# First norm of a hybrid decoder trunk: column sums and the modulation's shift with the data as the stationary operand, and eight load buffers of their own

## The chip, the cores and the metric

The kernel runs on one core of one Trainium2 chip. The metric is the device time of one execution in microseconds; the time before is the median of three runs. The core has five engines: TensorE (PE; PEld is its weight load), VectorE (DVE), ScalarE (ACT), GpSimd (POOL) and SyncE (SP), which issues most of the DMAs. Each works through its own instructions in a fixed order and waits on semaphores for the others.

## The reference, cut to what matters

A decoder trunk of two layers over a sequence of 1024 tokens with 1024 features. Layer 0 mixes with an S5 state space, layer 1 with Mamba-2; a squared-ReLU MLP follows each. Every sublayer starts with a norm and a modulation by a conditioning vector c:

```
def _rmsnorm(x, g):
    y = xf * lax.rsqrt(jnp.mean(xf * xf, axis=-1, keepdims=True) + NORM_EPS)
    return y * g
def _modulate(h, shift, scale):
    return h * (1 + scale) + shift
...
cond = jax.nn.silu(c)
mod = cond @ ada_w[i] + ada_b[i]
sh1, sc1, g1, sh2, sc2, g2 = jnp.split(mod[:, None, :], N_MOD, axis=-1)
h = _modulate(_rmsnorm(x, norm_mix_g[i]), sh1, sc1)
y = _s5_mixer(h, ...)
```

The change concerns the first `_rmsnorm` of layer 0, and `sh1` and `sc1` of its first `_modulate`.

## The kernel before, in words

Activations lie transposed: features on the 128 partitions, tokens along the free axis. x is eight tiles `x0[k]` of 128 features by 1024 tokens, each seen as two halves `x[k][f]` of 512 tokens.

The head of the program, up to the first projection, does this:

- `mod_rows` loads c on all partitions and makes `cond`; `mod_setup` makes `condc`, the same values with feature k*128+p in column k.
- `rstd_first` (L182) loads the eight x tiles, squares each half on ScalarE (L190) and sums over the partitions on TensorE (L191): the weight is `ones` (128x1), the 512 squares stream, and the result is one row per half, accumulated over k. `columns` (L337) then copies the two rows to SBUF (L341) and turns them into eight columns `pn` by eight products with one column (L344). VectorE makes `rfv` from them (L194), then the inverse root in some dozen small operations (`rsqrt`, L137 to L143, tiles `rsi`, `rst`, `rfy`), and `spread` (L156) broadcasts the result over the partitions.
- `mod_block` (L306) makes the scale: eight rows `ada` of 512 KB are loaded (L332), each multiplied with `cond` and summed by one VectorE operation (L333, the dot). At its end stand `mod` (L316) and `G` (L322), the factor of the norm.
- `mod_shift` (L347) makes the shift: eight tiles `ada` from `in_ada0` (L354) stream through TensorE against a column of `condc` (L356) into two rows, and `columns` turns these into eight columns; L361 writes them to `K.mod`.
- Both load into the pool `raw` with four buffers, which c (`craw`), the first weights and other tiles use as well. The scale's loop runs ahead, and from its fifth step one step of the shift is taken for each step of the scale.
- Then x is scaled with G (L1516, 16 operations), and `shift_split` writes each of the 16 tiles h as a high part on ScalarE (L237) and the rest on VectorE (L238). x holds both halves until then.
- `s5_uproj` projects h with `s5_w_in`: each unit of weights is loaded (L95) and split into `whi` (ScalarE, L84) and `wlo` (VectorE, L85), and three products per block (L117 whi by h high, L118 whi by h low, L119 wlo by h high) go to TensorE. `s5_tables`, `s5_front` (L896 on VectorE; `dI` and `bb` are its first results; L945 and L946 on TensorE) and `s5_back` prepare the state space beside it.

The order of instructions on each engine isn't written by hand: a scheduler fixes it when the kernel is built, by its own model of the times, so that work from further down (the tables of the state space, such as `mag`, `q`, `R`) stands between the operations above. Once built, it doesn't change. Tiles take their buffers from pools, and a buffer that is still in use makes the next load wait.

Of the kernel before, what the change touches and what calls it, by code (L numbers as in the profile page):

```python
# [11 lines left out]
F32 = mybir.dt.float32  # L12
# [7 lines left out]
P = 128  # L20
# [3 lines left out]
KT = D // P  # L24
# [28 lines left out]
def half_of(half):  # L53
    return slice(half * HT, half * HT + HT)


def blk(i, n=P):
    return slice(i * n, i * n + n)
# [4 lines left out]

def psum(K):

    K.turn += 1
    i = K.turn % (6 if K.wide else 4)
    if i >= 4:
        return K.pw.tile([P, 512], F32, tag="pw", name="pd")
    return (K.ps if i < 2 or not K.psb else K.psb).tile([P, 512], F32, tag="ps", name="pd")  # L70


def psw(K):

    return K.pw.tile([P, 512], F32, tag="pw", name="pm")


def tmp(K, name):
    return K.tmp.tile([P, 512], F32, tag="t", bufs=6, name=name)
# [51 lines left out]
def rsqrt(K, y, v):  # L131

    V = K.nc.vector
    n = v.shape[1]
    i = K.tmp.tile([P, n], I32, tag="rsi", name="rsi")
    t = K.tmp.tile([P, n], F32, tag="rst", name="rst")
    V.tensor_scalar(i, v.bitcast(I32), 1, None, op0=ALU.logical_shift_right)  # L137
    V.tensor_scalar(i, i, -1, 0x5F3759DF, op0=ALU.mult, op1=ALU.add)
    yy = i.bitcast(F32)
    for _ in range(3):  # L140
        V.scalar_tensor_tensor(t, yy, -0.5, yy, op0=ALU.mult, op1=ALU.mult)
        V.tensor_tensor(t, t, v, op=ALU.mult)
        V.scalar_tensor_tensor(y, t, 1.5, yy, op0=ALU.add, op1=ALU.mult)  # L143
        yy = y


def pss(K):

    return K.pss.tile([P, 512], F32, tag="pss", name="pn")


def spread(K, y, bank=pss):

    pb = bank(K)
    for j in range(4):
        K.nc.tensor.matmul(pb[:, blk(j)], y[:, j:j + 1].to_broadcast([P, P]), K.ident, start=True, stop=True)  # L156
    return pb
# [23 lines left out]

def rstd_first(K, x, load):  # L182

    nc = K.nc
    pr = [psw(K), psw(K)]
    for k in range(KT):
        load(k)
        for f in range(2):
            sq = tmp(K, "sq")
            nc.scalar.activation(sq, x[k][f], AF.Square)  # L190
            nc.tensor.matmul(pr[f][0:1], K.ones, sq, start=k == 0, stop=k == KT - 1)  # L191
    pt = columns(K, pr, 8)
    v = K.tmp.tile([P, 8], F32, tag="rfv", name="rfv")
    nc.vector.tensor_scalar(v, pt[:, 0:8], 1.0 / D, EPS, op0=ALU.mult, op1=ALU.add)  # L194
    y = K.tmp.tile([P, 8], F32, tag="rfy", name="rfy")
    rsqrt(K, y, v)
    return [spread(K, y[:, f * 4:f * 4 + 4], psw) for f in range(2)]
# [36 lines left out]
def shift_split(K, t, h, sh):  # L234

    hi, lo = h
    K.nc.scalar.activation(hi, t, AF.Identity, bias=sh)  # L237
    K.nc.vector.scalar_tensor_tensor(lo, t, sh, hi.bitcast(F32), op0=ALU.add, op1=ALU.subtract)  # L238
# [8 lines left out]
def h_half(K, h, half):  # L247
    for k in range(KT):
        h[k][half] = (h_tile(K, k, half, 0), h_tile(K, k, half, 1))


def h_new():
    return [[None, None] for _ in range(KT)]
# [23 lines left out]
def drain(gen):  # L277
    for _ in gen:
        pass
# [26 lines left out]
def mod_block(K, ada, i, j):  # L306

    nc = K.nc
    o = i * 48 + j * 8
    acc = K.tmp.tile([P, 8], F32, tag="macc", name="macc")  # L310
    for k in range(8):
        mod_dot(K, ada[i, j * 8 + k], acc[:, k:k + 1])
        if k < 7:
            yield
    m = K.mod[:, o:o + 8]
    nc.vector.scalar_tensor_tensor(  # L316
        m, acc, 0.5, K.cst[:, C_ADAB + o:C_ADAB + o + 8], op0=ALU.mult, op1=ALU.add
    )
    if j in (1, 4):
        s = i * 2 + (j == 4)  # L320
        g0 = (C_GMLP if j == 4 else C_GMIX) + i * 8
        nc.vector.scalar_tensor_tensor(  # L322
            K.G[:, s * 8:s * 8 + 8], m, 1.0, K.cst[:, g0:g0 + 8], op0=ALU.add, op1=ALU.mult
        )
    yield


def mod_dot(K, w, acc):

    pool, bufs = (K.adap, 2) if K.adap else (K.raw, 4)  # L330
    r = pool.tile([P, 1024], F32, tag="ada" if K.adap else "raw", name="ada", bufs=bufs)
    K.nc.sync.dma_start(r, w)  # L332
    K.nc.vector.scalar_tensor_tensor(r, r, 1.0, K.cond, op0=ALU.mult, op1=ALU.mult, accum_out=acc)  # L333


def columns(K, rows, n):

    nc = K.nc
    row = K.wt.tile([P, 1024], F32, tag="whi", name="row")
    for f, r in enumerate(rows):  # L340
        nc.scalar.copy(row[0:1, half_of(f)], r[0:1])  # L341
    pt = pss(K)
    for j in range(n):
        nc.tensor.matmul(pt[:, j:j + 1], row[0:1, blk(j)], K.ones[0:1], start=True, stop=True)  # L344
    return pt


def mod_shift(K, w):

    nc = K.nc  # L350
    rows = [psum(K), psum(K)]
    for k in range(KT):
        r = K.raw.tile([P, 1024], F32, tag="raw", name="ada")
        nc.sync.dma_start(r, w[k])  # L354
        for f in range(2):
            nc.tensor.matmul(  # L356
                rows[f][0:1], K.condc[:, k:k + 1], r[:, half_of(f)], start=k == 0, stop=k == KT - 1
            )
        yield
    pt = columns(K, rows, 8)  # L360
    nc.vector.scalar_tensor_tensor(  # L361
        K.mod[:, 0:8], pt[:, 0:8], 0.5, K.cst[:, C_ADAB:C_ADAB + 8], op0=ALU.mult, op1=ALU.add
    )


def mod_gate(K, ada, k):

    V = K.nc.vector
    acc = K.tmp.tile([P, 1], F32, tag="mac1", name="mac1")
    mod_dot(K, ada[0, 16 + k], acc)  # L370
    m = K.mod[:, 16 + k:17 + k]
    V.scalar_tensor_tensor(m, acc, 0.5, K.cst[:, C_ADAB + 16 + k:C_ADAB + 17 + k], op0=ALU.mult, op1=ALU.add)
    V.tensor_scalar(K.g1h[:, k:k + 1], m, 0.5, None, op0=ALU.mult)
# [409 lines left out]
def s5_tables(K, keep, pool, Lm):  # L783
# [4 lines left out]

    nc, V, S = K.nc, K.nc.vector, SimpleNamespace()

# [3 lines left out]
    def KT_(nm, n=64):  # L794
        return keep.tile([P, n], F32, name=nm, tag=nm, bufs=1)
# [3 lines left out]
    for nm, top, bot in (("1", 0.25, 0.0), ("2", 0.5, 0.25)):  # L799
# [4 lines left out]
        o[nm] = (t, b)  # L804
    S.sgn, S.nsgn, S.quarter = KT_("sgn", 1), KT_("nsgn", 1), KT_("quarter", 1)
    V.memset(S.sgn[0:64], 1.0)
    V.memset(S.sgn[64:128], -1.0)
    V.tensor_scalar(S.nsgn, S.sgn, -TWO_PI, None, op0=ALU.mult)
    V.memset(S.quarter, TWO_PI / 4)

# [594 lines left out]
@with_exitstack  # L1405
def trunk(ctx: ExitStack, tc: tile.TileContext, io, out):
    nc = tc.nc
    K = SimpleNamespace(nc=nc, tc=tc, io=io, turn=-1, psb=None, wide=False, adap=None, nact=7)

    def perm(name, **kw):  # L1410
        return ctx.enter_context(tc.tile_pool(name=name, **kw))
# [26 lines left out]
    def right(name, n=1):  # L1438
        return tc.alloc_tile_pool(name=name, bufs=n, side="right", reuse_waits="tile")
# [62 lines left out]
    t5 = right("tab5")  # L1502
    Lm = t5.tile([P, 3, 64], F32, name="lam", tag="lam", bufs=1)
    nc.sync.dma_start(Lm, io.lam.rearrange("a p g -> p a g"))
    pb = rstd_first(K, x, lambda k: nc.sync.dma_start(x0[k], io.x[k]))
    shift, scale = mod_shift(K, io.ada0), mod_block(K, io.ada, 0, 1)
    for k in range(KT):
        next(scale)
        if k >= 4:
            next(shift)  # L1510
    drain(shift)
    h = h_new()
    for f in range(2):
        h_half(K, h, f)
        for k in range(KT):
            nc.vector.scalar_tensor_tensor(x[k][f], x[k][f], K.G[:, k:k + 1], pb[f], op0=ALU.mult, op1=ALU.mult)  # L1516
        for k in range(KT):
            shift_split(K, x[k][f], h[k][f], K.mod[:, k:k + 1])
    S = s5_tables(K, keep5, t5, Lm)
    t5.release()  # L1520
    xp.release()
# [107 lines left out]
    pr = ssd_proj(K, cp, h, 0)  # L1629
# [27 lines left out]
    for gr in range(1, 4):  # L1657
        pr = ssd_proj(K, cp, h_mix, gr)
# [123 lines left out]
```

## Time and profile before

| | |
|---|---|
| median of three runs | 2531.93 us (2530.64 to 2536.54) |
| profiled execution, its own time | 2533.94 us |
| span of its profile | 2532.2 us |
| mean granted TensorE clock | 0.986 |
| PE busy | 2451.7 us (97%) |
| DVE busy | 1914.6 us (76%) |
| ACT busy | 1167.9 us (46%) |
| DMA | 503.80 MB, mean 199 GB/s |

Times in the profile's rows are microseconds from the start of the span. A row of the timeline has start, duration, engine, line, operation, what it writes and reads, shapes and count, and in brackets the idle time of the engine before it and what ended it. In the chain of work that ended last each row has start, duration and what the chain went through. Matmuls are pipelined and their ends are modelled, so the distance between starts tells more of the pace than a duration does. An f32 product appears as two passes. The granted clock (PEclk) is 1.00 at full speed and 0.50 at half.

### The profile page before, as it was taken

To read this page: it belongs to the slowest core of one execution; us is meant where nothing else is said; L and a number is where in the kernel's file an instruction comes from. 1 tells how busy PE (TensorE), PEld (TensorE's weight loads), DVE (VectorE), ACT (ScalarE), POOL (GpSimd) and SP (SyncE) were. 2 spreads that over 40 slices of the span, in tenths; PEclk is the share of its full clock that TensorE was granted. 3 is DMA by queue.
4 is the path that set the end of the run, shared out by engine and by line. 5 is a ranking of instruction groups with operands and counts; after the bars stand their busy time and mean duration, and the time that the engine had idled before them with its cause. 6 is when DMAs were issued, how large, how long until landed. Compare 5 with 4: busy or idle time off the path is not lost.

```text
span 2532.2 us, 32780 instructions
## 1 busy us (share of the span) xinstructions
PE 2451.7 (97%) x11624; PEld 1965.7 (78%) x11624; DVE 1914.6 (76%) x3265; ACT 1167.9 (46%) x1955; POOL 213.7 (8%) x400
## 2 busy tenths in 40 slices
PE   7999999999998999999999999999999999899997
PEld 2788788877776888777888878778888777688886
DVE  8798754967887997958596868789687777776664
ACT  4587412744444433534564655544255444444342
POOL 0010000112221000100000000000011222200000
PEclk9999999999999999999999999999999999999998
DMA  6576772467769979723455554584245666874752
GB/s 243 155 169 169 242 242 96 153 204 250 258 227 343 342 260 308 272 85 115 154 160 160 161 173 139 169 259 136 88 141 192 225 231 232 294 250 136 254 194 77
DMA packets 284645, 503.80 MB, mean 199 GB/s; under 512 B 22081, under 2 KB 162369, under 8 KB 284481
## 3 DMA queue, kind: packets, MB, share of 16 engines
q1 hardware_dynamic: 242496, 386.34, 47.3%
q0 software_dynamic: 32384, 106.98, 12.4%
q10 hardware_dynamic: 9600, 8.39, 1.0%
q8 instruction: 91, 1.49, 0.2%
q14 instruction: 74, 0.60, 0.1%
HBM read 364.27 MB, written 133.17 MB: 196 GB/s over the span
## 4 chain that ended last, share of the span: by engine, by line
PE 74%; issue 8%; DVE 6%; DMA 6%; ACT 4%; POOL 2%; SPq 0%; DVEq 0%; POOLq 0%; ACTq 0%
PE pd L118 10%; PE pd L117 10%; PE pd L119 10%; PE py L117 4%; PE py L118 4%; PE py L119 4%; PE px L117 3%; PE pm L117 2%; PE pm L118 2%; PE pm L119 2%; PE px L119 2%; PE px L118 2%; PE pv L117 2%; PE pv L118 2%; PE pv L119 2%
## 5 line engine op out<-in xcount | busy, mean ns | idle before, releaser
L84 ACT CAST whi<-raw 128x1024 fp32r<-128x1024 f32 x241 | 251.0, 1048 | 365.5 <-PE pd L118 146.3
L85 DVE TENSOR_TENSOR wlo<-raw,whi 128x1024 fp32r<-128x1024 f32 x241 | 293.2, 1218 | 113.6 <-ACT whi L84 110.2
L333 DVE SCALAR_TENSOR_TENSOR ada<-ada,cond 128x1024 f32<-128x1024 f32 x88 | 107.3, 1222 | 57.8 <-DMA ada<-in_ada 57.7
L498 ACT ACTIVATE s<-s 128x512 f32<-128x512 f32 x84 | 53.0, 631 | 158.5 <-DVE s L496 155.9
L390 POOL DMA_DIRECT2D hscr<-x x32 | 17.3, 541 | 953.6 <-DVE x L736 751.1
L1235 DVE SCALAR_TENSOR_TENSOR cacc<-cr,conv,cacc 128x1024 f32<-128x1024 f32 x72 | 91.7, 1279 | 0.9 <-ACT cacc L1216 0.8
L1288 ACT ACTIVATE L<-csb,cs 128x128 f32<-128x128 f32 x224 | 69.9, 391 | 38.4 <-DMA csb<-csr 33.7
L505 POOL DMA_DIRECT2D b<-s x96 | 51.8, 540 | 330.9 <-ACT s L499 281.7
L496 DVE TENSOR_TENSOR s<-s,px 128x512 f32<-128x512 f32 x60 | 41.0, 684 | 34.9 <-PE px L119 34.9
L496 DVE TENSOR_TENSOR s<-s,pv 128x512 f32<-128x512 f32 x36 | 24.7, 686 | 55.5 <-PE pv L119 55.5
L505 POOL DMA_DIRECT2D b<-tt x96 | 51.8, 540 | 43.0 <-DVE tt L510 25.8
L499 ACT ACTIVATE s<-s 128x512 f32<-128x512 f32 x84 | 53.2, 633 | 2.7
L1239 ACT ACTIVATE cth<-cacc 128x512 f32<-128x512 f32 x48 | 27.7, 625 | 41.4 <-DVE cacc L1235 41.3
L667 DVE SCALAR_TENSOR_TENSOR x<-py,mod,x 128x512 f32<-128x512 f32 x40 | 27.3, 744 | 25.6 <-PE py L119 25.6
L1215 ACT COPY cr<-pd 128x512 f32<-128x512 f32 x48 | 27.8, 579 | 35.0 <-PE pd L119 35.0
L1308 DVE SCALAR_TENSOR_TENSOR y<-xs,cst,pm 128x128 f32<-128x128 f32 x128 | 38.3, 342 | 4.8 <-PE pm L1305 4.8
L117 PE MATMUL pd<-h00h,whi 128*128 128x512 f32 (+1 forms) x97 | 39.7, 411 | 2.0 <-ACT h00h L237 1.8
L1106 ACT ACTIVATE gt<-pd,bgh 128x512 f32<-128x512 f32 x16 | 11.0, 685 | 65.5 <-PE pd L119 65.5
L117 PE MATMUL pd<-h01h,whi 128*128 128x512 f32 x97 | 39.4, 407 | 0.5 <-DVE h61h L736 0.5
L119 PE MATMUL pd<-h10h,wlo 128*128 128x512 f32 (+1 forms) x97 | 39.3, 405 | 0.0
L622 DVE TENSOR_TENSOR raw<-raw 128x1024 f32<-128x1024 f32 x16 | 19.6, 1225 | 26.0 <-DMA raw<-in_w 26.0
L118 PE MATMUL pd<-h00l,whi 128*128 128x512 f32 (+1 forms) x97 | 38.8, 400 | 0.4 <-DVE h00l L238 0.4
(996 smaller groups left out, 8173.0 us busy)
## 6 DMA issues: line engine op xcount, KB each, us to landing
raw<-in_w SPq DMA_DIRECT2D x204, 512.0 KB, 4.6
br<-b SPq DMA_DIRECT2D x112, 512.0 KB, 4.7
ada<-in_ada SPq DMA_DIRECT2D x96, 512.0 KB, 5.0
b<-s POOLq DMA_DIRECT2D x96, 256.0 KB, 2.9
b<-tt POOLq DMA_DIRECT2D x96, 256.0 KB, 3.8
csb<-csr SPq DMA_DIRECT2D x32, 512.0 KB, 4.5
raw<-in_w_xbc SPq DMA_DIRECT2D x24, 512.0 KB, 4.5
xscr<-cacc SPq DMA_DIRECT2D x24, 512.0 KB, 2.7
```

The source lines that it names most:

```text
L84: K.nc.scalar.copy(hi, src)
L85: K.nc.vector.tensor_tensor(lo, src, hi.bitcast(F32), op=ALU.subtract)
L117: K.nc.tensor.matmul(ps, wh, xh, start=start and i == 0, stop=False, skip_group_check=more)
L118: K.nc.tensor.matmul(ps, wh, xl, start=False, stop=False, skip_group_check=more)
L119: K.nc.tensor.matmul(ps, wl, xh, start=False, stop=stop and i == n - 1, skip_group_check=more)
L333: K.nc.vector.scalar_tensor_tensor(r, r, 1.0, K.cond, op0=ALU.mult, op1=ALU.mult, accum_out=acc)
L496: nc.vector.tensor_tensor(t, t, p, op=ALU.add)
L498: nc.scalar.activation(t, t, AF.Relu)
L499: nc.scalar.activation(t, t, AF.Square)
L505: self.K.nc.gpsimd.dma_start(self.bscr[DOWN.index(nm)][m // 2][m % 2], t)
L1235: V.scalar_tensor_tensor(acc, cr[:, t:t + L], K.cw[:, i, t:t + 1], acc, op0=ALU.mult, op1=ALU.add)
L1288: nc.scalar.activation(Lm[:, r, :], cb[:, r, :], AF.Relu, bias=S.cs[:, c0 + r:c0 + r + 1], scale=-1.0)
```

## The change

Three things change.

- `rstd_first` and `mod_shift` use the data as the stationary operand. `column` multiplies a 128x128 block of the squares (or of `ada`) as the weight with one moving column (`ones`, or a column of `condc`), and accumulates directly into a column of one PSUM tile `pn`. There are 64 such products in each place where there were 16. The rows, their copies and the function `columns` go.
- A pool `md` with eight buffers takes the loads of the scale and of the shift, in place of the four of `raw`. It stands on the right-hand stack above `tab5` and is released when h is made.
- The scale is now made whole, and then the shift, in place of the mixed loop.

```diff
-    pr = [psw(K), psw(K)]
+    pt = pss(K)
     for k in range(KT):
         load(k)
         for f in range(2):
             sq = tmp(K, "sq")
             nc.scalar.activation(sq, x[k][f], AF.Square)
-            nc.tensor.matmul(pr[f][0:1], K.ones, sq, start=k == 0, stop=k == KT - 1)
-    pt = columns(K, pr, 8)
+            for j in range(4):
+                column(K, pt, f * 4 + j, sq[:, blk(j)], K.ones, k == 0 and f == 0 and j == 0, k == KT - 1)
...
-    pool, bufs = (K.adap, 2) if K.adap else (K.raw, 4)
+    pool, bufs = (K.adap, K.nada) if K.adap else (K.raw, 4)
...
-def columns(K, rows, n):
+def column(K, pt, j, w, v, first, last):
+
+    K.nc.tensor.matmul(pt[:, j:j + 1], w, v, start=first, stop=last, skip_group_check=True)
...
-    rows = [psum(K), psum(K)]
+    pt = pss(K)
     for k in range(KT):
-        r = K.raw.tile([P, 1024], F32, tag="raw", name="ada")
+        r = K.adap.tile([P, 1024], F32, tag="ada", name="ada", bufs=K.nada)
         nc.sync.dma_start(r, w[k])
-        for f in range(2):
-            nc.tensor.matmul(
-                rows[f][0:1], K.condc[:, k:k + 1], r[:, half_of(f)], start=k == 0, stop=k == KT - 1
-            )
+        for j in range(KT):
+            column(K, pt, j, r[:, blk(j)], K.condc[:, k:k + 1], k == 0 and j == 0, k == KT - 1)
         yield
-    pt = columns(K, rows, 8)
...
+    K.adap, K.nada = right("md"), 8
     pb = rstd_first(K, x, lambda k: nc.sync.dma_start(x0[k], io.x[k]))
-    shift, scale = mod_shift(K, io.ada0), mod_block(K, io.ada, 0, 1)
-    for k in range(KT):
-        next(scale)
-        if k >= 4:
-            next(shift)
-    drain(shift)
+    drain(mod_block(K, io.ada, 0, 1))
+    drain(mod_shift(K, io.ada0))
...
+    K.adap.release()
+    K.adap, K.nada = None, 2
```

The scheduler lays the instructions anew. On TensorE, at the start of the program (`pm`, `pn`, `pd` are PSUM tiles; each row is one product or a run of them):

```order
L191 MATMUL pm<-sq,ones 1x512 x16
L344 MATMUL pn<-ones,row 128x1 x8
L356 MATMUL pd<-ada,condc 1x512 x3
L156 MATMUL pm<-ident,rfy 128x128 x8
L356 MATMUL pd<-ada,condc 1x512 x13
L344 MATMUL pn<-ones,row 128x1 x8
L117 MATMUL pd<-h00h,whi 128x512
L118 MATMUL pd<-h00l,whi 128x512
```

and in the changed kernel:

```order
L339 MATMUL pn<-ones,sq 128x1 x64
L156 MATMUL pm<-ident,rfy 128x128 x8
L339 MATMUL pn<-condc,ada 128x1 x64
L117 MATMUL pd<-h00h,whi 128x512
L118 MATMUL pd<-h00l,whi 128x512
L117 MATMUL pd<-h01h,whi 128x512
L118 MATMUL pd<-h01l,whi 128x512
L119 MATMUL pd<-h00h,wlo 128x512
```

The sums and the shift are 64 products with one column each (L339, one line for both), all of the shift stands behind the spread (L156), and the first projection takes the two halves' whi products ahead of the first product with wlo.

On VectorE, where the first dot stands (L333, L334 in the changed kernel), before:

```order
L333 SCALAR_TENSOR_TENSOR ada,macc<-ada,cond 128x1024
L833 TENSOR_TENSOR mag<-mag,ea_e_559 128x64
L880 TENSOR_TENSOR q_644<-nr,lam 128x64
L833 TENSOR_TENSOR mag<-mag,ea_e_559 128x64
L333 SCALAR_TENSOR_TENSOR ada,macc<-ada,cond 128x1024
L833 TENSOR_TENSOR mag<-mag,ea_e_559 128x64
L881 TENSOR_TENSOR qt_645<-ni,lam 128x64
L833 TENSOR_TENSOR mag<-mag,ea_e_559 128x64
L882 TENSOR_TENSOR q_644<-q_644,qt_645 128x64
L333 SCALAR_TENSOR_TENSOR ada,macc<-ada,cond 128x1024
L833 TENSOR_TENSOR mag<-mag,ea_e_559 128x64
```

and in the changed kernel:

```order
L334 SCALAR_TENSOR_TENSOR ada,macc<-ada,cond 128x1024
L195 TENSOR_SCALAR rfv<-pn 128x8
L824 TENSOR_TENSOR mag<-mag,ea_e_633 128x64
L137 TENSOR_SCALAR rsi<-rfv 128x8
L871 TENSOR_TENSOR q_718<-nr,lam 128x64
L138 TENSOR_SCALAR rsi<-rsi 128x8
L334 SCALAR_TENSOR_TENSOR ada,macc<-ada,cond 128x1024
L141 SCALAR_TENSOR_TENSOR rst<-rsi 128x8
L824 TENSOR_TENSOR mag<-mag,ea_e_633 128x64
L142 TENSOR_TENSOR rst<-rst,rfv 128x8
L872 TENSOR_TENSOR qt_719<-ni,lam 128x64
L143 SCALAR_TENSOR_TENSOR rfy<-rst,rsi 128x8
```

`rfv`, which reads the sums, moved from behind the third dot to right behind the first; the other seven dots stand behind it, and the operations of the inverse root between them.

On ScalarE, from the last squares on, before:

```order
L190 ACTIVATE sq<-x_247 128x512 x2
L341 COPY row<-pm 1x512 x2
L341 COPY row<-pd 1x512
L84 CAST whi<-raw 128x1024
L341 COPY row<-pd 1x512
L84 CAST whi<-raw 128x1024
L237 ACTIVATE h00h<-x_240,mod 128x512
L237 ACTIVATE h10h<-x_241,mod 128x512
```

and in the changed kernel, from the last high parts of h on:

```order
L238 ACTIVATE h51h<-x_245,mod 128x512
L238 ACTIVATE h61h<-x_246,mod 128x512
L238 ACTIVATE h71h<-x_247,mod 128x512
L84 CAST whi<-raw 128x1024 x2
L982 ACTIVATE tph<-iota,phi 128x128 x8
L918 COPY F_824<-BC 64x128
```

The two casts `whi` of the projection's first weights moved from ahead of the 16 high parts of h to behind them; the four row copies are gone. The first two `wlo` on VectorE stand behind the last low part of h as well, where one of them stood ahead of the first.

SyncE issues the eight loads of the scale and then the eight of the shift; before, it issued five of the scale, then shift and scale in turn, and five of the shift at the end. What it issues next (`s5d`, two `raw`, two `kscr`) stands as before.

More of the change, by code (lines that the diff above doesn't have):

```diff
@@ L333, in mod_dot @@
     K.nc.vector.scalar_tensor_tensor(r, r, 1.0, K.cond, op0=ALU.mult, op1=ALU.mult, accum_out=acc)
-def columns(K, rows, n):
[L338 to L345, printed above, removed]
+def column(K, pt, j, w, v, first, last):
+    K.nc.tensor.matmul(pt[:, j:j + 1], w, v, start=first, stop=last, skip_group_check=True)
 def mod_shift(K, w):
     nc = K.nc
-    rows = [psum(K), psum(K)]
+    pt = pss(K)
     for k in range(KT):
-        r = K.raw.tile([P, 1024], F32, tag="raw", name="ada")
+        r = K.adap.tile([P, 1024], F32, tag="ada", name="ada", bufs=K.nada)
         nc.sync.dma_start(r, w[k])
-        for f in range(2):
-            nc.tensor.matmul(
-                rows[f][0:1], K.condc[:, k:k + 1], r[:, half_of(f)], start=k == 0, stop=k == KT - 1
-            )
+        for j in range(KT):
+            column(K, pt, j, r[:, blk(j)], K.condc[:, k:k + 1], k == 0 and j == 0, k == KT - 1)
         yield
-    pt = columns(K, rows, 8)
     nc.vector.scalar_tensor_tensor(
@@ L1407, in trunk @@
     nc = tc.nc
-    K = SimpleNamespace(nc=nc, tc=tc, io=io, turn=-1, psb=None, wide=False, adap=None, nact=7)
+    K = SimpleNamespace(nc=nc, tc=tc, io=io, turn=-1, psb=None, wide=False, adap=None, nada=2, nact=7)
     def perm(name, **kw):
```

## The prediction

> **What bounds the kernel now.** I read the chain of work that ended last first, because only what stands on it costs time, and only its first 60 us, because the change touches nothing later by its own lines. Columns: start us, us, what.
>
> ```profile
> 24.76 4.63 DMA ada<-in_ada
> 29.52 3.59 PE pd L356 x4
> 33.13 6.03 DMA ada<-in_ada
> 39.20 1.89 PE pd L356 x4
> 41.10 4.72 DMA ada<-in_ada
> 45.87 4.47 PE pd L356 x10
> 51.88 0.48 ACT row L341
> 52.41 1.06 PE pn L344 x8
> 55.45 0.68 DVE h00l L238
> 56.17 0.79 PE pd L118
> ```
>
> From 24.76 to 53.5 the chain belongs to the shift: its loads, which come one by one because their buffers come free late, and its products (L356), then the row copies and columns (L341, L344). Then h is made and TensorE starts the input projection, in earnest at 56.17. Behind that, windows of 10 us (engine busy time and count for PE, PEld, DVE, ACT, POOL; granted clock; DMA share; GB/s):
>
> ```profile
> 100.00:110.00 10.00, 7.70 (x35) 6.02 (x34) 10.00 (x23) 6.82 (x15) 0.51 (x1) 0.84 0.98 246
> 110.00:120.00 10.00, 10.00 (x60) 7.57 (x59) 8.02 (x18) 5.53 (x9) 0.00 (x0) 0.99 0.28 95
> 190.00:200.00 10.00, 10.00 (x67) 8.90 (x66) 10.00 (x25) 7.84 (x13) 1.60 (x3) 1.00 0.96 209
> ```
>
> Apart from 2.3 us of idleness around 105, TensorE is full. So the head is worth what it moves the start of the projection on TensorE, less what a later start can fill up again.
>
> **What the products cost.** Old and new products move the same data through TensorE in opposite roles. The old ones stream 512 columns against a one-column weight:
>
> ```profile
> 8.27 15.38 PE L191 MATMUL pm<-sq,ones 128*1 128x512 f32 x32 [8.27 <-ACT sq L190]
> 9.93 0.13 PEld L191 LDWEIGHTS pm<-sq,ones 128*1 128x1 f32 x1 [0.72 <-issue]
> 10.78 0.13 PEld L191 LDWEIGHTS pm<-sq,ones 128*1 128x1 f32 x1 [0.72 <-ACT sq L190]
> 11.90 0.08 PEld L191 LDWEIGHTS pm<-sq,ones 128*1 128x1 f32 x1 [0.34 <-issue]
> 12.33 0.08 PEld L191 LDWEIGHTS pm<-sq,ones 128*1 128x1 f32 x1 [0.34 <-issue]
> ```
>
> Each f32 product is two passes (32 for 16). A pass starts 0.85 us after the last at first (9.93 to 10.78) and 0.43 us after it once the clock is up (11.90 to 12.33). The new form, a 128x128 weight and one column moving, is already in the later norms:
>
> ```profile
> 434.70 1.05 PE L173 MATMUL pn<-ones,ss 128*128 128x1 f32 x8 [0.37 <-DVE ss L170]
> 2516.85 1.87 PE L215 MATMUL pn<-ones,ss 128*128 128x1 f32 x8 [3.83 <-DVE ss L210]
> 2516.66:2520.07 3.41, 1.87 (x8) 1.78 (x8) 1.25 (x8) 0.00 (x0) 0.00 (x0) 0.50 0.00 0
> ```
>
> Eight passes end after 1.05 us at full clock and 1.87 us where the window shows a clock of 0.50. Less the tail of the last pass (about 0.19 and 0.16), that is 0.107 and 0.214 us a pass. The change puts four times as many passes (128 for 32, twice), each a quarter as long: **at equal clock the work is equal**, 13.7 us each time at full clock and 27.4 us at half. So the clock decides. These are windows of 3.41 us, laid where the clock changes:
>
> ```profile
> 24.95:28.36 3.41, 0.57 (x6) 0.48 (x5) 3.41 (x11) 0.00 (x0) 0.00 (x0) 1.00 0.77 238
> 28.36:31.77 3.41, 2.25 (x3) 0.37 (x4) 3.37 (x15) 0.00 (x0) 0.00 (x0) 0.50 0.92 296
> 31.77:35.19 3.42, 3.23 (x5) 0.19 (x3) 2.16 (x10) 0.00 (x0) 0.00 (x0) 0.50 0.70 235
> 38.60:42.01 3.41, 2.14 (x5) 0.34 (x6) 1.50 (x4) 0.00 (x0) 0.00 (x0) 1.00 0.77 255
> 55.67:59.08 3.41, 3.00 (x8) 2.33 (x8) 3.41 (x6) 3.41 (x7) 0.00 (x0) 0.50 0.00 0
> ```
>
> A window with PE busy 0.57 is followed by half clock; 2.25 leaves it there; 3.23 and 3.00 lift it. In these windows it is passes of 512 columns that lift it. No row shows whether a long run of one-column passes does: with 128x128 weights, eight is the longest run. That is the unknown, with both ends measured per pass. I take **half clock**. In a one-column pass hardly anything streams; the time goes into the weight load. And the nearest row is the one at 2516.85: it starts after idleness, with no streaming beside it, as here, and ran at half clock (though its 1.87 us in the window would not have been enough by the rows above either way).
>
> [...]
>
> **The sum at half clock.** Rows of VectorE and ScalarE:
>
> ```profile
> 21.88 1.22 DVE L333 SCALAR_TENSOR_TENSOR ada<-ada,cond 128x1024 f32<-128x1024 f32 x1
> 23.02 0.27 DVE L833 TENSOR_TENSOR mag<-mag,ea_e 128x64 f32<-128x64 f32 x1
> 23.51 1.21 DVE L333 SCALAR_TENSOR_TENSOR ada<-ada,cond 128x1024 f32<-128x1024 f32 x1
> 33.69 0.17 DVE L143 SCALAR_TENSOR_TENSOR rfy<-rst,rfy 128x8 f32<-128x8 f32 x1
> 42.19 9.97 DVE L1516 SCALAR_TENSOR_TENSOR x<-x,G,pm 128x512 f32<-128x512 f32 x15
> 53.49 0.17 DVE L361 SCALAR_TENSOR_TENSOR mod<-pn,cst 128x8 f32<-128x8 f32 x1 [1.33 <-PE pn L344]
> 54.23 1.22 DVE L85 TENSOR_TENSOR wlo<-raw,whi 128x1024 fp32r<-128x1024 f32 x1
> 55.37 0.75 DVE L238 SCALAR_TENSOR_TENSOR h00l<-x,mod,h00h 128x512 fp32r<-128x512 f32 x1
> 65.31 0.75 DVE L238 SCALAR_TENSOR_TENSOR h71l<-x,mod,h71h 128x512 fp32r<-128x512 f32 x1
> 67.10 0.27 DVE L896 TENSOR_TENSOR dI<-ident,s5d 16x128 f32<-16x128 f32 x1
> 50.84 1.04 ACT L84 CAST whi<-raw 128x1024 fp32r<-128x1024 f32 x1
> 54.49 0.72 ACT L237 ACTIVATE h00h<-x,mod 128x512 fp32r<-128x512 f32 x1
> 63.70 0.71 ACT L237 ACTIVATE h71h<-x,mod 128x512 fp32r<-128x512 f32 x1
> ```
>
> 1. Sums: 8.27 + 128 x 0.214 = 35.7, against 23.65 (8.27 + 15.38) before. The row copies and columns behind them (L341, L344) go. ScalarE's squares now wait for TensorE (six buffers), and so does the first dot behind them, by some 2 us; the wait in step 2 hides both.
> 2. VectorE's rfv now stands right behind the first product with the condition (the dot), and is a wait: the seven other dots queue behind it from about 25 to 35.8. Until rfy follow 4 dots of 1.14 us (21.88 to 23.02) and 19 small ones of 0.16 (three from 23.02 to 23.51): 7.6 us, 43.4. Up to G it is the old stretch 21.88 to 33.86 (12.0 us, six dots), one dot longer, with 0.5 us (an estimate, four small operations) for mod and G: 13.6 us, 49.4.
> 3. Spread (L156), 16 passes of 128 columns at half clock, priced as the one-column pass: 3.4 us, 46.8.
> 4. Shift: 128 x 0.214 = 27.4, ending at 74.2. The scaling of x (15 in 9.97 us) ends at 59 and hides. The last dot ends by 48 and frees the last buffer; its load lands by 53 (4.63 us as in the chain), well before its passes at 71. So the eight buffers hide, and gain nothing here. mod at 74.3.
> 5. ScalarE makes all 16 h tiles, now ahead of both weight casts: 15 x 0.614 (54.49 to 63.70) + 0.6 + 1.0 = 10.8, first projection pass at 85.1. VectorE's 16 (0.663 each, 55.37 to 65.31) and the first wlo (1.22) end at 87. Four passes fit ahead of that wait where one did, worth 1.3 us. So TensorE's real start goes from 56.17 to about 85.7: **+29.5**. VectorE's next stage (dI) goes from 67.10 to 88: +21.
> 6. Given back: 2.3 us of idleness near 105 and, in the same row, 16% of lost clock over 10 us, 1.6 us: -4.
>
> Together +25.5 on the profiled 2533.94 us: 2559.4. The median of the three runs stands 2.0 lower, so **2557**. Ends: if VectorE's delay alone counted and 4 us more were filled up, +17 (2549); with nothing given back, +29.5 (2561). Behind 110 the schedule is also shuffled; with a full TensorE I cost that at nothing, 1 us either way.
>
> **Rivals.**
> *Full clock (W).* If one-column passes count as work, sums end at 23.7 as before, rfv follows at 23.8, rfy at 31.4, G at 37.4. TensorE has been idle since 23.7, so spread runs at half clock to 34.8. The shift is bound by its passes: 4 at half clock, then 0.107 each, 49.0. Loads keep up:
>
> ```profile
> 18.00:20.00 2.00, 2.00 (x6) 0.34 (x4) 1.90 (x8) 1.16 (x3) 0.00 (x0) 1.00 1.01 404
> ```
>
> At 404 GB/s a row of 0.52 MB takes 1.3 us; the first is there for the dot at 21.88, so seven more are by 31, and the last dot (36.9) plus 4.63 is 41.5. mod at 49.1 is 4.4 us earlier than 53.49, but the late casts and the wlo eat it: wlo at 61.9, less 1.3, is +4.4 on TensorE, less the 4 given back: about 0, **2532** (2528 to 2538). For it: TensorE's rows are unbroken in this form. Against it: nothing shows such a run lifting the clock. [...]
>
> *VectorE sets the pace (V).* As W, but behind the projection's start VectorE binds (the 10.00 at 190): its dI comes at 62.9, 4.2 us early, and the shuffled order keeps that and 1 to 2 us of the idleness: **2526**. Against it: TensorE is as full in the same row.
>
> *The change does less than it says.* The order shows eight loads and then eight issued in a row, and no copies, so it does; only that loads cease to matter is sure.
>
> **How the numbers follow.** Half clock 0.56, W 0.34, V 0.10. About 0.2% (5 us) can be told from no change. Slower: 0.54 of half clock and 0.08 of W's upper end, 0.62. Same: the rest of W and 0.02, 0.27. Faster: V and a little of W, 0.11. W is too likely to leave out, so the range runs from 2530, inside W, to 2562; the forecast's own is 2549 to 2562.
>
> **What would show it.** Right: the one-column passes 0.21 us apart from 8.3 to 36 and for some 27 us behind the spread, granted clock 0.50 there; rfv waiting about 12 us; mod near 74; whi behind h71h; first projection pass near 85. Wrong: passes 0.107 apart from about 11.3, sums done by 24, mod near 49. If mod comes at 74 and the time hardly moves, my belief in a full TensorE behind it is what failed.

## The result, and the profile after

| | before | after |
|---|---|---|
| median | 2531.78 us (2530.64 to 2536.54, 4 runs) | 2555.54 us (2553.89 to 2558.74, 4 runs) |
| ratio to before | 1 | 1.0094, 95% interval 1.0077 to 1.0111 |
| profiled execution, its own time | 2533.94 us | 2556.86 us |
| span of its profile | 2532.2 us | 2555.1 us |
| mean granted clock | 0.986 | 0.983 |

The changed kernel is 0.9% slower. A second set of runs (e10 below) gave 2557.6 us, ratio 1.0101 (1.0083 to 1.0118).

TensorE's timeline of the changed kernel, its head (start, duration, engine, line, what; L339 is the line of every one-column product, L156 the spread, L117 and L119 the first projection):

```profile
9.35 27.47 PE L339 MATMUL pn<-ones,sq 128*128 128x1 f32 x128 [9.35 <-ACT sq L191]
43.69 3.75 PE L156 MATMUL pm<-ident,rfy 128*128 128x128 f32 x16 [6.87 <-DVE rfy L143]
47.23 24.20 PE L339 MATMUL pn<-condc,ada 128*128 128x1 f32 x128
82.58 0.80 PE L117 MATMUL pd<-h00h,whi 128*128 128x512 f32 x1 [11.14 <-ACT whi L84]
84.45 0.79 PE L119 MATMUL pd<-h00h,wlo 128*128 128x512 f32 x1
```

The sums' 128 passes take 27.47 us, 0.215 apiece; the 32 long passes before took 15.38. The shift takes 24.20 us, all of it behind the spread. Then TensorE stands for 11 us until the weight cast arrives. VectorE's timeline of the same kernel shows the two waits and when the next stage (the tables, whose first operation writes dI) is reached:

```profile
36.86 0.17 DVE L195 TENSOR_SCALAR rfv<-pn 128x8 f32<-128x8 f32 x1 [11.05 <-PE pn L339]
49.01 0.16 DVE L323 SCALAR_TENSOR_TENSOR G<-mod,cst 128x8 f32<-128x8 f32 x1
71.48 0.17 DVE L352 SCALAR_TENSOR_TENSOR mod<-pn,cst 128x8 f32<-128x8 f32 x1 [12.07 <-PE pn L339]
82.38 0.74 DVE L239 SCALAR_TENSOR_TENSOR h71l<-x,mod,h71h 128x512 fp32r<-128x512 f32 x1
83.18 2.35 DVE L85 TENSOR_TENSOR wlo<-raw,whi 128x1024 fp32r<-128x1024 f32 x2
85.45 0.27 DVE L887 TENSOR_TENSOR dI<-ident,s5d 16x128 f32<-16x128 f32 x1
```

Before, rfv waited for nothing, mod came at 53.49 and dI at 67.10. In the chain of work that ended last (start, duration, what), no transfer stands between the first x and the projection any more, where three loads of the shift stood before:

```profile
8.67 0.64 ACT sq L191
9.35 27.48 PE pn L339 x128
...
43.69 3.75 PE pm L156 x16
47.44 24.01 PE pn L339 x128
71.48 0.18 DVE mod L352
...
81.59 0.94 ACT whi L84
82.58 0.80 PE pd L117
```

So the eight buffers did take the loads off the path, and TensorE's own passes took their place. Windows of one microsecond of the same kernel (width; busy time and count for PE, PEld, DVE, ACT, POOL; granted clock; DMA share; GB/s) show what the passes did to the clock:

```profile
46.00:47.00 1.00, 1.00 (x6) 1.00 (x6) 1.00 (x3) 0.00 (x0) 0.00 (x0) 1.00 1.02 385
47.00:48.00 1.00, 1.00 (x8) 1.00 (x6) 1.00 (x2) 0.00 (x0) 0.00 (x0) 1.00 0.79 315
48.00:49.00 1.00, 1.00 (x11) 1.00 (x10) 1.00 (x5) 0.00 (x0) 0.00 (x0) 1.00 0.75 266
50.00:51.00 1.00, 1.00 (x11) 1.00 (x10) 1.00 (x3) 0.00 (x0) 0.00 (x0) 1.00 0.85 283
51.00:52.00 1.00, 1.00 (x8) 1.00 (x8) 1.00 (x2) 0.00 (x0) 0.00 (x0) 0.67 0.90 307
52.00:53.00 1.00, 1.00 (x7) 1.00 (x6) 1.00 (x3) 0.00 (x0) 0.00 (x0) 0.50 0.88 318
```

Count the passes, not the busy time; a pass that reaches into a window from either side is in its count. Up to 48 the spread's passes, and from 47.2 the shift's first ones, run at half pace: the counts are six to eight, and four to six passes start in a microsecond. From 48 to 51 the count is eleven and nine start, 0.112 us apart: the full pace. From 51.3 the granted clock reads 0.50 and four or five start, 0.213 us apart. TensorE is busy 1.00 throughout: it lost its clock while it never paused. (The column reads 1.00 ahead of the first recorded change of the clock, at 47.93, although the sums went at 0.215 us a pass and the spread at 0.22, half pace; there the count is the better witness.)

A landmark far behind the head helps to see what is carried on: the last start of the gate's activation (gt), the second of the two times in these rows, before and then after:

```profile
L1106 ACT ACTIVATE gt<-pd,bgh x16: 677/687/691, 294.5 to 450.5; 128x512 f32<-128x512 f32 x16
L1097 ACT ACTIVATE gt<-pd,bgh x16: 679/691/692, 316.7 to 472.1; 128x512 f32<-128x512 f32 x16
```

It comes 21.6 us later; from there to the end both need about the same (2081.7 and 2083.0 us). In the profiles below that rest lies between 2076 and 2095 us without a trend that I could tie to the head.

### The profile page after: what moved, and what is told of

Read it like the earlier page. It is cut to its first block, busy times and chain, and to the rows that moved or that the text cites. A ratio compares the mean times of both kernels' runs of the same rounds, so it can differ in the third digit from the quotient of the medians.

```text
span 2555.1 us, 33093 instructions
## 1 busy us (share of the span) xinstructions
PE 2462.2 (96%) x11784; PEld 2007.0 (79%) x11784; DVE 1915.2 (75%) x3265; ACT 1170.1 (46%) x1953; POOL 214.2 (8%) x400
## 4 chain that ended last, share of the span: by engine, by line
issue 42%; PE 36%; DVE 8%; DMA 7%; POOL 3%; ACT 3%; SPq 0%; POOLq 0%; DVEq 0%; ACTq 0%
PE py L117 3%; PE pd L117 3%; PE py L118 3%; PE pd L119 3%; PE py L119 3%; PE pd L118 3%; DMA ada<-in_ada 3%; POOL b L496 2%; DMA raw<-in_w 2%; PE pn L339 2%; PE px L117 2%; PE px L118 2%; PE px L119 2%; PE pm L118 1%; PE pm L119 1%
## 5 line engine op out<-in xcount | busy, mean ns | idle before, releaser
L334 DVE SCALAR_TENSOR_TENSOR ada<-ada,cond 128x1024 f32<-128x1024 f32 x88 | 107.3, 1222 | 50.7 <-DMA ada<-in_ada 50.4
L117 PE MATMUL pd<-h00h,whi 128*128 128x512 f32 (+1 forms) x97 | 40.7, 422 | 16.0 <-ACT whi L84 11.1
L658 DVE SCALAR_TENSOR_TENSOR x<-py,mod,x 128x512 f32<-128x512 f32 x40 | 27.3, 744 | 25.6 <-PE py L119 25.6
L117 PE MATMUL pd<-h01h,whi 128*128 128x512 f32 x97 | 39.8, 410 | 0.3 <-DVE h61h L727 0.3
L119 PE MATMUL pd<-h10h,wlo 128*128 128x512 f32 (+1 forms) x97 | 39.0, 402 | 0.0
L117 PE MATMUL pd<-h30h,whi 128*128 128x512 f32 (+1 forms) x97 | 38.0, 393 | 1.0 <-ACT h30h L1072 1.0
```

Of the source, the lines that this page charges most:

```text
L117: K.nc.tensor.matmul(ps, wh, xh, start=start and i == 0, stop=False, skip_group_check=more)
L119: K.nc.tensor.matmul(ps, wl, xh, start=False, stop=stop and i == n - 1, skip_group_check=more)
```

## The experiments

The theory, a guess that the runs below are to test: weight loads take nearly all of a one-column pass (PEld reads 1.00 in the rows from 48 to 53 above), and the clock goes with the moving columns and not with the weight loads, so the sums and the shift run at half pace. The rivals: the shuffled order or the buffers cost the time, or loading a 128x128 weight costs 0.21 us at any clock. Behind that a second question: which engine carries the delay on, TensorE, which starts the projection late, or VectorE, which comes late to the tables?

### e1: 128 columns in place of one

```diff
-    column(K, pt, f * 4 + j, sq[:, blk(j)], K.ones, ...)
+    column(K, pts, i, sq[:, blk(j)], K.ones.to_broadcast([P, 128]), ...)
...
-    column(K, pt, j, r[:, blk(j)], K.condc[:, k:k + 1], ...)
+    column(K, pts, j, r[:, blk(j)], K.condc[:, k:k + 1].to_broadcast([P, 128]), ...)
```

The diff is shortened: besides, the eight results lie in two PSUM tiles (`pts`), and VectorE copies one column of each into a small tile (`gcol`).

> Edit: the changed kernel, but each product moves 128 equal columns (ones or the condition's column broadcast) in place of one, into 128 equal columns of PSUM, of which one is read. Weight loads and the number of passes stay at 128 each time. Theory A (the clock counts streaming, not weight loads): passes 0.107 us apart from about 11.5 on, sums done by 25 in place of 36.8, shift ending near 50 in place of 71.4, time 2525 to 2534. Theory B (the loss comes from the loop order, the load buffers and rfv's place in the order, not from the clock): sums still end near 37 and the time stays at 2552 or above. Theory C (a weight load costs 0.214 us here whatever the clock): as B, passes stay 0.214 apart.

Measured: 2532.57 us, ratio 1.0008 (0.9998 to 1.0017). TensorE's timeline:

```profile
9.05 16.06 PE L342 MATMUL pn<-ones,sq 128*128 128x128 f32 x128 [9.05 <-DVE ea_r L759]
30.17 1.62 PE L342 MATMUL pn<-condc,ada 128*128 128x128 f32 x6 [5.05 <-DMA ada<-in_ada]
36.56 3.44 PE L156 MATMUL pm<-ident,rfy 128*128 128x128 f32 x16 [4.78 <-DVE q L886]
39.84 13.79 PE L342 MATMUL pn<-condc,ada 128*128 128x128 f32 x122
```

The same 128 weight loads, each with 128 times as many columns behind it, take 16.06 us in place of 27.47, and the shift goes at 0.113 us a pass (13.79 / 122). More work in less time: the weight load is not a fixed 0.21 us, and the buffers and their order are in this kernel as well. The sums' part stands in the same order on TensorE in both kernels, so there only the columns differ. The order behind it isn't the same: the two casts `whi` stand ahead of h here again, so the time as a whole holds more than the passes' pace. The kernel loses nothing any more, but gains nothing either: the spread waits for the inverse root until 36.56, and 122 of the shift's 128 passes stand behind it.

### e6: 64 columns

The same edit with 64 for 128.

> The changed kernel with 64 equal columns moving in each of its 64 + 64 products in place of one, and a copy that picks one column of each; nothing is left out. At full pace a pass with 128 moving columns took about 0.113 us, so 64 columns stream for half of a pass. Theory S (only streaming counts for the clock, and a share near one half is too little: the granted clock fell in the kernel before after stretches of 3.4 us with 1.83 us or less of TensorE work, and stayed with 2.14 or more): the sums go at 0.214 us a pass, 27 us in all, the clock is not lifted ahead of the spread, mod comes near 70, time 2550 to 2557. Theory L (any moving data beyond one column, or weight loads counted in part): the passes fall to 0.11 to 0.13 us, mod by 56, time 2530 to 2536.

Measured: 2549.84 us, ratio 1.0064 (1.004 to 1.0089), the four runs in two pairs, near 2542 and near 2557. TensorE's timeline, from the profile of one of the lower pair:

```profile
9.34 27.57 PE L342 MATMUL pn<-ones,sq 128*128 128x64 f32 x128 [9.34 <-DVE ea_p L761]
44.02 3.75 PE L156 MATMUL pm<-ident,rfy 128*128 128x128 f32 x16 [7.11 <-DVE q L887]
47.56 14.72 PE L342 MATMUL pn<-condc,ada 128*128 128x64 f32 x128
73.62 0.79 PE L117 MATMUL pd<-h00h,whi 128*128 128x512 f32 x1 [11.34 <-ACT whi L84]
```

Both theories were half right. 64 columns did not lift the clock in 27.57 us of sums (0.215 us a pass); behind the spread the same form kept the full pace for all of its 128 passes (0.115 apiece), where one column lost it after one stretch of 3.4 us. So 64 columns, by the expectation's estimate from e1's 0.113 us half a pass of streaming, kept a clock that they had not lifted. TensorE's order up to there is that of the changed kernel, so this is the columns' doing alone. In these three profiles the clock went with the number of moving columns: 128 lifted it (e1), 64 kept it, one did neither. What it counts, no profile shows. The two pairs lie about 15 us apart, and a shift at half pace would be 12.7 us longer (27.4 less 14.7); that the upper pair is runs in which the clock wasn't lifted would fit. Neither of them has a profile, but their mean granted clock on record points the same way: 0.992, against 0.990 in the lower pair. In the profile the first projection passes, behind TensorE's wait of 11.34 us, start 0.43 us apart up to 78.9 and 0.23 apart from there. In e10 below, where the head never lifted the clock, the column reads 1.00 over just such passes (from 55 to 120, with passes 0.43 us apart up to 89.4), and that makes a mean higher.

### e2, e3, e4: one half of the change at a time

e2 puts both products back into the old form and keeps the eight buffers and the order of the scale ahead of the shift; e3 puts back the sums alone, e4 the shift alone.

```diff
+    pr = [psw(K), psw(K)]
...
-            for j in range(4):
-                column(K, pt, f * 4 + j, sq[:, blk(j)], K.ones, ...)
+            nc.tensor.matmul(pr[f][0:1], K.ones, sq, start=k == 0, stop=k == KT - 1)
```

The excerpt shows the sums' part; the shift's products and `columns` come back likewise.

> Edit: both products back in the old form (data streams, rows, copies, columns); the eight buffers and the order scale first, shift second stay. Theory A: sums end near 24.5, the loads come earlier than in the kernel before, shift done near 47, time 2524 to 2531. Theory B: the buffers and the order are what cost, 2548 or above.

> Edit: only the norm's sums back in the old form, the shift with the data stationary and one column. Theory A: sums near 24.5, spread near 35, shift's passes fall to half clock one window after the spread and end near 59, casts still behind h, time 2540 to 2547. Theory B: 2550 or above.

> Edit: only the shift back in the old form, the sums with one column. Theory A: sums end near 37, spread near 47, shift at full clock 14 us and its columns 2 us, mod near 63.5, casts ahead of h, time 2534 to 2541. Theory B: 2550 or above.

| kernel | ratio to before (95%) | sums end | mod | dI | last gt |
|---|---|---|---|---|---|
| before | 1 | 23.7 | 53.49 | 67.10 | 450.5 |
| e2, both old | 1.0014 (1.0003 to 1.0026) | 25.8 | 56.63 | 69.49 | 456.2 |
| e3, shift changed | 1.0083 (1.0068 to 1.0098) | 25.4 | 64.20 | 79.78 | 464.0 |
| e4, sums changed | 1.0074 (1.005 to 1.0098) | 36.6 | 64.47 | 77.34 | 463.6 |
| changed | 1.0094 (1.0077 to 1.0111) | 36.8 | 71.48 | 85.45 | 472.1 |

All three came out slower than theory A had them: 2534.61, 2553.04 and 2549.69 us. e3 lies in theory B's range and e4 at its edge, but e2, which has the buffers and the order and neither new product, is far below it. So the buffers and the order are not the bulk of what costs; theory A had the sizes too small. At gt the parts nearly add up: against e2, the shift costs 7.8 us, the sums 7.4, both 15.9. The order and the buffers by themselves put gt 5.7 later (e2), which I had at nothing or a gain. The timeline of e2 on TensorE shows a part of it:

```profile
29.92 1.87 PE L362 MATMUL pd<-ada,condc 128*1 128x512 f32 x2 [2.27 <-DMA ada<-in_ada]
37.03 3.76 PE L156 MATMUL pm<-ident,rfy 128*128 128x128 f32 x16 [5.25 <-DVE rfy L143]
40.72 13.59 PE L362 MATMUL pd<-ada,condc 128*1 128x512 f32 x30
```

With the whole scale first, VectorE works through its eight dots with the root between them, the spread has to wait until 37.03, and 30 of the shift's 32 passes stand behind it. In the kernel before, six of them ran ahead of the spread, which stood there from 35.09 to 37.2, and the rest were done by 51.2; here they end at 54.3. That is 3 us of the 5.7, and not all of it need be the order's: e8 and e9 below keep the old head, and their mod comes at 53.46 and 55.25. In full times the parts do not add: e3 loses 21 us by its ratio, 13.5 of them by gt. Where the others arise behind gt, no run here shows.

### e5 and e11: TensorE earlier, VectorE not

The changed kernel with the first unit's casts ahead of the shifted tiles, run twice, the second time beside the changed kernel itself (e10).

```diff
+    first = unit(K, io.s5_w_in[0])
     h = h_new()
...
-    up = s5_uproj(K, h, io.s5_w_in)
+    up = s5_uproj(K, h, io.s5_w_in, first)
```

> The changed kernel, except that the first projection unit's load and casts are put ahead of the 16 shifted tiles; nothing is left out. The sums and the shift stay as slow as they are in the changed kernel (mod near 71.5). TensorE's first projection passes can then start when the first shifted tiles are there, near 75 instead of 82.6 to 84.5; VectorE does the same instructions as before it reaches the tables (dI), so dI stays near 85.4. Theory V (what comes after 85 hangs on when VectorE gets to the tables, not on when TensorE starts): 2553 to 2557, the last of the gate passes (gt) starting near 472 as in the changed kernel. Theory P (TensorE's late start is carried to the end, as the prediction had it): 7 to 9 us faster, 2545 to 2549, gt near 464.

> The changed kernel once more, on one chip with its version that casts first, to tell those two apart by more runs. If the clock's windows stand as in its first profile, the shift takes 24 us and mod comes near 71.5; if the spread falls into two windows so that it lifts none, the shift takes 27.4 and mod comes near 74. Time as in its first runs, 2553 to 2558.

> The changed kernel with the first unit's casts ahead of the shifted tiles, once more. Its first four runs spread from 2545.6 to 2555.4. Theory V (TensorE's earlier start is worth nothing): within 3 us of the changed kernel on the same chip. Theory P: 7 to 9 us faster than that. Both in part: 3 to 7 us faster.

Measured: e5 2547.39 us, 1.0053 (1.0038 to 1.0067); side by side, e10 2557.6, 1.0101 (1.0083 to 1.0118), and e11 2554.38, 1.0077 (1.0059 to 1.0094). TensorE's timeline of e10 and then of e11:

```profile
9.16 27.46 PE L339 MATMUL pn<-ones,sq 128*128 128x1 f32 x128 [9.16 <-DVE ea_r L746]
43.49 3.75 PE L156 MATMUL pm<-ident,rfy 128*128 128x128 f32 x16 [6.87 <-DVE rfy L143]
47.04 27.30 PE L339 MATMUL pn<-condc,ada 128*128 128x1 f32 x128
85.48 0.79 PE L117 MATMUL pd<-h00h,whi 128*128 128x512 f32 x1 [11.13 <-ACT whi L84]
```

```profile
47.16 27.31 PE L339 MATMUL pn<-condc,ada 128*128 128x1 f32 x128
77.02 0.80 PE L117 MATMUL pd<-h00h,whi 128*128 128x512 f32 x1 [2.56 <-ACT whi L84]
```

Here the shift took the full 27.3 us: the same spread lifted nothing. In the traces of the kernel before and of the changed kernel the recorded changes of the granted clock, 26 and 16 of them, lie whole multiples of 3.41 us apart (in the changed kernel the first are at 47.93, 51.34 and 88.89). So I counted windows of 3.41 us back: in that profile from its first change, in the others, as an estimate, from where the starts of the first projection passes go from 0.43 to 0.23 us apart (89.4 in e10, 83.3 in e11, 81.7 in e5, 82.3 in e3, 60.0 in e1, 78.9 in e6). In the first profile the spread fills 2.92 us of the last window before the clock rises. In e10 it falls into two windows, with 1.59 and 2.17 us of it, in e11 with 2.12 and 1.64. Where one-column passes or nothing stood beside it, the passes went at full pace behind a spread with 2.92 us or more of it in a window (the first profile and e1) and not with 2.60 or less (e3, e5, e10, e11); in e6, with 64-column passes beside it, 2.96 us was enough as well. So in these seven profiles the pace at which the shift started went with how the spread fell against these windows, and with it the 3 us that the shift saved in the first.

TensorE starts 8.5 us earlier in e11, dI stands at 88.35 in e10 and 88.55 in e11, and the last gt at 473.8 and 473.2: up to there the earlier start is worth 0.6 us, as theory V had it (e5's profile has gt at 473.0). In the times it is worth 3.2 us in one comparison, with intervals that overlap, at the lower edge of "both in part", and about 0.4% between the changed kernel's first runs and e5, each against its own runs of the kernel before; e5's median lies in theory P's range. The ten runs of this version fall into five at 2545.6 to 2548.3 and five at 2554.1 to 2555.4; both profiles are of the upper five.

The mean granted clock on record says more. It was 0.983 in the first profile, where the spread lifted the clock and the rest of the head then read 0.50, and 0.990 in the profiles of e5, e10 and e11, where it did not (27.3 us of shift) and the head, in e10 and e11 from 55 to 120, read 1.00. The lower five runs have 0.984 to 0.986, the upper five 0.990 but for one (0.985). So the lower five are probably runs in which the spread lifted the clock; why they are 8 us faster, where the shift saves 3, stays open. Among the runs of e10 and e11 with 0.990 or more, the earlier start is worth about 3 us (2554.1 to 2555.3 against 2557.4 to 2564.6).

### e8 and e9: each engine late alone

Both start from the kernel before. e8 puts 27 operations on a scratch tile ahead of the tables on VectorE; e9 puts 86 extra passes ahead of the first projection pass on TensorE. In e8 zero times the scratch tile is added to `q`, so that the tables have to wait for it; the first part of the excerpt is e8's, the second e9's.

```diff
+    z = tmp(K, "zz")
+    lo = h[7][1][1].bitcast(F32)
+    nc.vector.tensor_tensor(z, lo, lo, op=ALU.max)
+    for _ in range(26):
+        nc.vector.tensor_tensor(z, z, z, op=ALU.max)
+    for q in S.q:
+        nc.vector.scalar_tensor_tensor(q, z[:, 0:64], 0.0, q, op0=ALU.mult, op1=ALU.add)
...
+    for _ in range(K.late):
+        K.nc.tensor.matmul(p, wh[:, blk(0)], h[0][half][0], start=True, stop=True)
```

> The kernel before, with 27 extra operations on a 128x512 scratch tile (0.6 us apiece, 16 us in all) put on VectorE between the shifted tiles and the tables, which wait for them; nothing is left out, and TensorE's first projection passes stay at 55 to 56. It delays VectorE alone. Theory V (VectorE's arrival at the tables is carried to the end): 13 to 17 us slower than the kernel before, 2545 to 2549, the last gate pass (gt) near 464 instead of 450.5. Theory P (only TensorE's start counts): at most 4 us slower, under 2536.

> The kernel before, with 86 extra single passes of 512 columns (0.227 us apiece, 19.5 us in all) put on TensorE ahead of the first projection pass, which then overwrites their bank; nothing is left out, and VectorE reaches the tables (dI) near 67 as before. It delays TensorE alone. Theory P (TensorE is full from 56 on, so its late start is carried to the end): 16 to 20 us slower than the kernel before, 2547 to 2552. Theory V (TensorE waits for VectorE later in this stage, and takes most of the delay out of those waits): at most 6 us slower, under 2538, the last gate pass near 452 to 456.

Measured: e8 2556.18 us, 1.0097 (1.0076 to 1.0118); e9 2563.92 us, 1.0125 (1.0104 to 1.0145). VectorE's timeline of e8 and TensorE's of e9:

```profile
67.07 0.68 DVE L1522 TENSOR_TENSOR zz<-h71l 128x512 f32<-128x512 f32 x1
93.35 0.27 DVE L896 TENSOR_TENSOR dI<-ident,s5d 16x128 f32<-16x128 f32 x1
```

```profile
57.01 21.39 PE L128 MATMUL pd<-h00h,whi 128*128 128x512 f32 x86 [1.80 <-ACT h00h L241]
78.24 0.39 PE L117 MATMUL pd<-h00h,whi 128*128 128x512 f32 x1
```

In e8 dI came 26 us late, more than the 16 us put in, because the scheduler set about 7 us of later table work between the extra operations; TensorE's projection began at 55.23 as before. The last gt came at 474.0, 23.5 late. In e9 TensorE's first pass came 23 us late and VectorE's dI at 68.86; the last gt came at 472.7, 22.2 late. The times moved by some 25 and 32 us; the ten that e9 lost beyond gt no run here explains. Both theories in their pure form are refuted: up to gt, either engine's delay alone is carried on nearly whole, and the other engine waits. The windows say it for e8 (same columns as above; 85 to 120 us, the kernel before and then e8):

```profile
85.00:120.00 35.00, 32.67 (x183) 24.70 (x183) 29.48 (x60) 20.80 (x45) 2.51 (x4) 0.95 0.68 169
```

```profile
85.00:120.00 35.00, 21.27 (x132) 16.64 (x133) 31.57 (x71) 11.16 (x23) 3.93 (x7) 0.69 0.43 110
```

TensorE, with no delay of its own, is busy for 21 of 35 us where it was for 33, and its clock falls to 0.69; one wait of 17.65 us, up to 96.78, ends with VectorE's `ET`, of the tables. In e9 it is VectorE that is busy less, from 120 to 200 for 60.22 us where it was for 73.77.

The two engines meet where TensorE starts the first product that reads the tables (`pn` from `F` and `ET`), at 74.75 in the kernel before. It comes 22.0 us later in the changed kernel, 23.8 in e10, 22.4 in e11, 22.0 in e8, and within 3 us of gt's own move in every profile but e9's, where it moved by 14.5 and gt by 22.2.

### e7: a version that gains

The 128-column kernel, with the spread placed behind the shift's first two blocks.

```diff
     drain(mod_block(K, io.ada, 0, 1))
-    drain(mod_shift(K, io.ada0))
+    shift = mod_shift(K, io.ada0)
+    for _ in range(2):
+        next(shift)
+    pb = [spread(K, y[:, f * 4:f * 4 + 4], psw) for f in range(2)]
+    drain(shift)
```

> The 128-column kernel, with the spread of the norm's reciprocal roots placed behind the shift's first two blocks (16 products, 32 passes) in place of behind three products; nothing is left out. In the 128-column kernel TensorE stood from 31.8 to 36.6 waiting for the roots with shift blocks in SBUF, and the shift's other 122 passes stood behind the spread until 53.6. Here some 26 more passes (about 3 us) are done in that gap, so the shift ends near 50, mod near 50.3, the first projection pass near 51.5, and VectorE reaches the tables (dI) near 62 (65.4 there, 67.1 in the kernel before). Theory V (VectorE's arrival at the tables is carried to the end): 3 to 5 us faster than the kernel before, 2526 to 2529. Rival (the start is made up later, or the spread comes 1 to 2 us later and takes it back): 2530 to 2533.

Measured: 2528.56 us over 12 runs against 2532.82 over 17, ratio 0.9986 (0.9975 to 0.9996): faster than both kernels, by a seventh of a percent over the one before (the interval runs from 0.04 to 0.25), and in theory V's range. TensorE's timeline:

```profile
30.79 6.40 PE L342 MATMUL pn<-condc,ada 128*128 128x128 f32 x32 [5.44 <-DMA ada<-in_ada]
37.03 1.95 PE L156 MATMUL pm<-ident,rfy 128*128 128x128 f32 x16
38.82 10.88 PE L342 MATMUL pn<-condc,ada 128*128 128x128 f32 x96
```

The gap ahead of the spread is filled, the spread waits for nothing and runs at full pace (1.95 us for 3.44), the shift ends at 49.7, dI comes at 62.83 (67.10 before) and the last gt at 448.3 (450.5). TensorE starts the projection 3.0 us earlier as well (52.24 for 55.26), so this version doesn't tell the two engines apart.

## Why the prediction was right, step by step

Its likeliest case came true, on the first unknown that it named: a long run of one-column passes neither lifted the clock (0.215 us a pass over the sums' 27.47 us) nor kept it (0.50 from 51.34 on). Its steps against the two profiles of the changed kernel (us from the span's start):

| step | predicted | first profile | e10 |
|---|---|---|---|
| 1 sums end | 35.7 | 36.8 | 36.6 |
| 2 spread can start | 43.4 | 43.69 | 43.49 |
| 2 G | 49.4 | 49.01 | 48.82 |
| 3 spread ends | 46.8 | 47.4 | 47.2 |
| 4 shift ends | 74.2 | 71.4 | 74.3 |
| 4 mod | 74.3 | 71.48 | 74.38 |
| 5 first projection pass | 85.1 | 82.58 | 85.48 |
| 5 dI | 88 | 85.45 | 88.35 |
| time of that execution | 2559.4 | 2556.86 | 2564.6 |

- **Step 1.** The pace was right (0.215 for 0.214). The first product came at 9.35 and 9.16 instead of 8.27; e8 and e9, which keep the old loads, have 9.06 and 9.72, so that is scatter and no cost of the buffers.
- **Step 2.** The wait of rfv was 11.05 us, and the seven dots did queue behind it. Both ends of this step came within 0.6 us.
- **Steps 3 and 4.** Right in e10 to 0.4 us. In the first profile the spread, 128 columns a pass, lifted the clock for one stretch of 3.4 us, and the shift saved 3. The prediction priced the spread's time, but did not ask whether it lifts the clock for what follows.
- **Step 4, the buffers.** "Hide, and gain nothing" was right of the loads. What it left out is that the buffers and the order that came with them have a price of their own where the shift is fast: e2 loses 5.7 us at gt and 0.14% (0.03 to 0.26) in time.
- **Step 5.** The late casts and the start of TensorE came as worked out, less the 3 us in the first profile.
- **Step 6 is the weak one.** It carried TensorE's +29.5 on and took 4 off for idleness filled up. The runs show another bookkeeping. The last gt moved by 21.6 and 23.3 us: less than TensorE's own delay at the first projection pass (27.3 and 30.2) and 2 to 3 more than VectorE's at dI (18.4 and 21.3). Starting TensorE 8.5 us earlier with VectorE unchanged moved gt by 0.6. So for the changed kernel the "VectorE's delay alone" that the prediction kept as its lower end was the nearer mechanism. But TensorE is no bystander: late alone, it carried 22 of 23 us to gt (e9). How two delays that come together make one, no run shows; it is not their sum.
- **Luck in the total.** It held because two sums lie close: 25.5 us predicted, and 22.9 between the two profiled executions, 23.8 and 26.4 between the medians. The reading behind it was also too broad: besides the 2.3 us near 105, TensorE in the kernel before stands idle for 7.0 us between 200 and 290 (busy for 83.01 of 90), which the step left out. That TensorE is nearly full up to there stood; that it alone sets what follows did not.
- **The rivals.** W (full clock) fell with the first row of the trace. V, whose condition was a full clock, is what e1 and e7 then made true with 128 columns: dI 4.3 us early in e7, the time 3.5 us less by the ratio; the prediction had 4.2 and, with the shuffled order, 6. Whether VectorE alone gave that, as V has it, e7 leaves open.

## What to carry to other kernels

A product turned round so that the data is the weight and one column moves had the same price on paper, but its passes kept TensorE occupied without keeping its clock (busy 1.00 at a granted clock of 0.50 from 52 to 53); ask of each long run how many columns a pass moves, and pad the moving side (128 columns lifted the clock here, and cost hardly more than one, at 0.113 us a pass) if the run starts at half clock. When loads are taken off a path, look at what then stands in a row on the engine: here the whole shift moved behind a spread that had to wait. And where two engines hand work to and fro, put the delay of each at the point where they meet, before carrying either to the end.

## What the hardware showed that I had not expected

- TensorE's clock fell at 51.3 us in the middle of a run without a gap, and the starts of its passes went from 0.112 to 0.213 us apart, with one column a pass. With 64 columns the clock stayed once it was up (14.72 us for 128 passes) and was not lifted from below (27.57 us for 128); with 128 columns it was lifted (16.06 us for 128, the start at half pace included).
- A pass with 128 columns took hardly longer than one with a single column at the same clock: 0.113 us in e1 against 0.107 (the kernel before) to 0.112 (the changed kernel) at full clock.
- The clock column of the profile reads 1.00 before its first recorded change, while passes already go at half pace (0.215 us each from 9.35 to 36.8).
- The same 16 passes of the spread lifted the clock for 3.4 us in one profile of the changed kernel and not in another. The clock changes in the traces of both kernels lie whole multiples of 3.41 us apart; the spread had 2.92 us in one such window in the first profile, and at most 2.17, by an estimate from the pace of the projection's passes, in the second (e10).
